# A hybrid encoder layer on one core: the stores of the local attention's output issued by POOL instead of SP

## The chip, the core and the metric

The kernel runs on one core of one Trainium2 chip. The metric is the device time of one launch in microseconds (us), as the median of several runs. The engines are named as the profile names them: PE (TensorE; PEld is its weight load), DVE (VectorE), ACT (ScalarE), POOL (GpSimd) and SP (SyncE). Each engine works through its own list of instructions in the order in which they stand there, and waits at one whose semaphores have not come.

## The reference, cut to what matters

One layer of an encoder over 1024 tokens of width 1024, in float32. A mixer made of a windowed softmax attention and a bidirectional gated delta rule is followed by a cross-attention into 256 memory tokens and a SwiGLU block, each between norms and with a residual:

```python
proj = h @ w_in                                   # h = rms_norm(x)
aq, ak, av, dqkv, dgate, dalpha, dbeta = split(proj)
attn_o = _window_attention(rope(aq), rope(ak), av, sink)   # 8 heads of 64, 2 kv heads, +-128 tokens
dn_o = _gated_deltanet(dqkv, dgate, dalpha, dbeta, ...)    # 4 heads, two directions, a scan over chunks
mix = concat([attn_o, dn_o], -1) @ w_out
x = x + rms_norm(mix)
x = x + rms_norm(cross_attention(rms_norm(x), rms_norm(mem)))
x = x + rms_norm(swiglu(rms_norm(x)))
```

The change touches `attn_o` on its way to the product with `w_out`.

## The kernel before, in words

Everything is computed transposed, with channels on the partitions, and matrices that do not fit are kept in DRAM scratch (names beginning with `d_`). Precision comes from splitting each float32 operand into a rounded high part and a rest (`split`, L103 on ACT and L104 on DVE or POOL) and multiplying three times.

The program is written as stages whose steps are interleaved by three lists of tokens. `ORDER_1` makes keys, queries and values of the delta rule and what its scan needs (`d_kv`, `d_pz`). `ORDER_2` makes the attention's queries and keys (L795, L797, into `d_q` and `d_k`) and begins the windows. `ORDER_3` runs the delta scan: `s01` is one quarter-by-quarter step of the two scans `scan(0)` and `scan(1)`, one for each pair of heads; `W` calls `next_windows`; `K` and `V` project the memory tokens. Then come the output projection (`mid_gemm`, L1104) over the first and the second half of the tokens, the cross-attention and the SwiGLU block.

A window is one token tile n of 128 tokens and one group g of four heads, 16 in all. `window(n, g)` is a generator in two halves. Its first half loads the tile's queries twice (`qr`, L674, SP), rounds them (`qs`, L676, ACT), replaces the lower 64 partitions by the rest (L677, POOL), multiplies with up to three key blocks (`psw`, L685, PE), adds the band and takes the row maximum (`sc`, `m`, L687, DVE), takes the exponential (L694, ACT), makes the sink's share (`es`, L697 on POOL, L698 on ACT, L699 and L700 on DVE) and scales (`sc`, L703 on DVE; in five of the windows L705 on ACT). The second half transposes (`ptw`, L711, PE), splits (`ph`, `pl`), multiplies with the values (`pow`, L716, PE), joins the two halves (`ao`, L719 on ACT, L720 on DVE) and stores the result to its place in `d_mix` (L721). `next_windows` runs the first half of one window, and then the second half of the one before. There is one `ao` tile and one `qr` tile.

A step of the scan loads `kv` (512 KB a direction, L858) and `pz` (L859) on SP, and runs products on PE (`psc`, L843) between which DVE updates `kv` (L871), `vg` (L878) and the state `S` (L891). From the fifth step on POOL adds and scales the two directions' outputs (`ol`, L920 to L930); `gate` (L918) is loaded and `osq` stored to `d_mix` (L940) on SP. In `next_keys` POOL makes the low part of the weights (`wlo`, L104). The output projection reads `d_mix` back (L1146).

All DMAs but the eight stores of `d_gate` (L817, ACT) are issued by SP. What stands behind what on an engine is not written by hand: a list scheduler goes through the recorded program with its own estimate of durations and places each instruction on its engine's list. DMAs issued by SP rotate through eight semaphores, so that each waits for the one issued eight before it.

Of the kernel before, what the change touches and what calls it, by code (L numbers as in the profile page):

```python
# [76 lines left out]
def tile_hybrid_block(  # L77
# [6 lines left out]
    nc = tc.nc  # L84
# [9 lines left out]
    def f32(ap):  # L94
        return ap.bitcast(F32)
# [4 lines left out]
    def split(hi, lo, src, scale=None, eng=None):  # L100

        if scale is None:
            nc.scalar.copy(hi, src)  # L103
            return (eng or nc.vector).tensor_tensor(lo, src, f32(hi), ALU.subtract)  # L104
        nc.scalar.activation(hi, src, AF.Identity, scale=scale)
        return nc.vector.scalar_tensor_tensor(lo, src, scale, f32(hi), ALU.mult, ALU.subtract)
# [83 lines left out]
    d_mix = dram.tile([D, S], F32, name="d_mix")  # L190
# [32 lines left out]
    for hf in range(2):  # L223
# [12 lines left out]
        for k in range(KT):  # L236
# [3 lines left out]
            g = gcol[:, k:k + 1]  # L240
# [422 lines left out]
    def window(n, g):  # L663

        tok = slice(n * P, (n + 1) * P)
        k0, k1 = max(n - 1, 0), min(n + 1, NT - 1) + 1
        nb = k1 - k0
        w = nb * P
        band = C[:, _AT["band0"] - C0 + (k0 - n + 1) * P:][:, 0:w]

        khi, klo = (t[:, k0 * P:k1 * P] for t in keys[g])
        qr = tw.tile([P, 4, P], F32, tag="qr", name="qr", bufs=1)
        for r in range(2):
            nc.sync.dma_start(qr[64 * r:64 * r + 64], d_q[256 * g:256 * g + 256, tok].rearrange("(h e) t -> e h t", h=4))  # L674
        qs = tw.tile([P, 4, P], F32R, tag="qs", name="qs")
        nc.scalar.copy(qs, qr)  # L676
        nc.gpsimd.tensor_tensor(qs[64:128], qr[64:128], f32(qs[64:128]), ALU.subtract)  # L677

        m4 = tw.tile([P, 4], F32, tag="m4", name="m4")
        ssum = tw.tile([P, 4], F32, tag="ssum", name="ssum")  # L680
        pr = []
        for hh in range(4):
            pp = pw.tile([P, 512], F32, tag="pw", name="psw")
            for i, kk in enumerate((khi, klo)):
                nc.tensor.matmul(pp[:, 0:w], qs[:, hh, :], kk, start=(i == 0), stop=(i == 1))  # L685
            sc = tw.tile([P, 384], F32, tag="sc", name="sc", bufs=8)
            nc.vector.tensor_tensor_reduce(out=sc[:, 0:w], in0=pp[:, 0:w], in1=band, scale=0.125,  # L687
                                           scalar=sink[:, 4 * g + hh:4 * g + hh + 1], op0=ALU.add, op1=ALU.max,
                                           accum_out=m4[:, hh:hh + 1])
            pr.append(sc)  # L690
        nm = tw.tile([P, 4], F32, tag="nm", name="nm")
        nc.vector.tensor_scalar(nm, m4, -1.0, None, ALU.mult)
        for hh in range(4):
            nc.scalar.activation(pr[hh][:, 0:w], pr[hh][:, 0:w], AF.Exp, bias=nm[:, hh:hh + 1],  # L694
                                 accum_out=ssum[:, hh:hh + 1])
        es = tw.tile([P, 4], F32, tag="es", name="es")
        nc.gpsimd.tensor_tensor(es, sink[:, 4 * g:4 * g + 4], m4, ALU.subtract)  # L697
        nc.scalar.activation(es, es, AF.Exp)  # L698
        nc.vector.tensor_tensor(es, es, ssum, ALU.add)  # L699
        nc.vector.reciprocal(es, es)  # L700
        for hh in range(4):
            if not 8 <= g * NT + n < 13:
                nc.vector.tensor_scalar(pr[hh][:, 0:w], pr[hh][:, 0:w], es[:, hh:hh + 1], None, ALU.mult)  # L703
            else:
                nc.scalar.mul(pr[hh][:, 0:w], pr[hh][:, 0:w], es[:, hh:hh + 1])  # L705
        yield
        po = pw.tile([P, 4, P], F32, tag="pow", name="pow", bufs=1)
        for j in range(nb):
            pp = pw.tile([P, 512], F32, tag="pw", name="ptw")
            for hh in range(4):  # L710
                nc.tensor.transpose(pp[:, hh * P:(hh + 1) * P], pr[hh][:, j * P:(j + 1) * P], ident)  # L711
            ph = tw.tile([P, 512], F32R, tag="ph", name="ph")
            pl = tw.tile([P, 512], F32R, tag="pl", name="pl")
            split(ph, pl, pp)
            for i, pe_ in enumerate((ph, pl)):
                nc.tensor.matmul(po.rearrange("p h t -> p (h t)"), vhl[:, k0 + j, g].rearrange("p r e -> p (r e)"), pe_,  # L716
                                 start=(j == 0 and i == 0), stop=(j == nb - 1 and i == 1))
        ao = tw.tile([P, 4, P], F32, tag="ao", name="ao", bufs=1)[0:64]
        nc.scalar.copy(ao, po[64:128])  # L719
        nc.vector.tensor_tensor(ao, po[0:64], ao, ALU.add)  # L720
        nc.sync.dma_start(d_mix[g * 256:(g + 1) * 256, tok].rearrange("(h e) t -> e h t", e=64), ao)  # L721

# [9 lines left out]
    def next_windows():  # L734

        for _ in range(2):
            last = wins[-1] if wins else None
            if wins_done[0] % NT == 0 and wins_done[0] < 2 * NT:
                window_keys(wins_done[0] // NT)
            if wins_done[0] < 2 * NT:  # L740
                wins.append(window(wins_done[0] % NT, wins_done[0] // NT))
                next(wins[-1])
            wins_done[0] += 1
            if last:
                next(last, None)
# [1131 lines left out]
```

## Time and profile before

| | |
|---|---|
| runs | 1518.25, 1521.06, 1524.97 us; median 1521.06 |
| profiled execution | 1518.84 us, of which the profile's span is 1516.8 us; mean granted clock of PE 0.996 |
| busy, share of the span | PE 97%, PEld 82%, DVE 73%, ACT 52%, POOL 24% |
| DMA | 256 MB in all, 169 GB/s on average; SP's queue 252.9 MB, ACT's 2.1 MB |

A row of the timeline has the start and the length in us, engine, line, operation and tiles; a number in brackets is how long the engine stood idle before it, with what released it. SPq is SP's queue of DMA issues: such a row is the issue, not the transfer. "Waits" rows give the idle time in total, the number of times and the longest. A busy PE is not a PE at its peak, since the ends of pipelined matmuls are modelled. The row of a stretch of the span has its start and end, its length, then the busy time of PE, PEld, DVE, ACT and POOL with the number of instructions in brackets, the clock granted to PE, the mean busy share of the 16 DMA engines, and GB/s.

### The profile page before, as it was taken

The numbers are of one execution on the slowest core, as the hardware profiler recorded it, in microseconds if no ns is written. First come the engines' busy times: TensorE is split into PE (matmuls) and PEld (weight loads), VectorE is DVE, ScalarE is ACT, GpSimd is POOL, SyncE is SP. The second block draws the span as 40 slices with busy tenths as digits, with TensorE's granted clock in tenths as the row PEclk, the third lists the DMA queues.
The fourth block names the chain that finished last, engine by engine and source line by source line (L and its number), as shares of the span: only waits on it lengthen the run. The fifth ranks groups of instructions, "written<-read, shape, count | busy, mean of one in ns | idle before, by whom it ended". The sixth has DMA issues, their size and how long they took to land.

```text
span 1516.8 us, 21323 instructions
## 1 busy us (share of the span) xinstructions
PE 1471.5 (97%) x7437; PEld 1239.2 (82%) x7437; DVE 1101.3 (73%) x1801; ACT 784.2 (52%) x1606; POOL 362.8 (24%) x394
## 2 busy tenths in 40 slices
PE   7999999998999999999999998999999999999998
PEld 6888877888989878887788876888888888888787
DVE  5878998676998775538466867776867764696666
ACT  7678844567556764555454684332332332453533
POOL 0011232432325303342201002433524342000030
PEclk9999999999999999999999999999999999999999
DMA  6245554557987584448625553334434333853255
GB/s 203 70 118 142 148 164 129 157 171 193 345 283 234 180 293 158 162 151 262 232 90 180 194 190 123 118 119 132 132 112 152 126 103 116 323 207 97 105 179 168
DMA packets 257751, 256.34 MB, mean 169 GB/s; under 512 B 18128, under 2 KB 190317, under 8 KB 257645
## 3 DMA queue, kind: packets, MB, share of 16 engines
q1 hardware_dynamic: 256493, 252.90, 52.3%
q10 hardware_dynamic: 1152, 2.10, 0.4%
q8 instruction: 58, 0.95, 0.3%
q14 instruction: 48, 0.39, 0.1%
HBM read 178.63 MB, written 73.70 MB: 166 GB/s over the span
## 4 chain that ended last, share of the span: by engine, by line
PE 64%; DVE 8%; DMA 5%; ACT 2%; issue 2%; POOL 1%; SPq 0%; DVEq 0%; ACTq 0%; POOLq 0%
PE pE L1514 8%; PE pD L1514 8%; PE pA L1514 6%; PE pmg L1104 6%; PE pdX L1720 6%; PE pst L1320 5%; PE pdA L1720 4%; PE pB L1514 4%; PE pcq L276 3%; PE psc L843 2%; PE pdD L1720 2%; DMA wpart<-in_w_co_dram 1%; PE pg L276 1%; DMA kv<-d_kv 1%; PE pcv L999 1%
## 5 line engine op out<-in xcount | busy, mean ns | idle before, releaser
L103 ACT CAST whi<-wraw 128x1024 fp32r<-128x1024 f32 x96 | 100.8, 1050 | 120.3 <-DMA wraw<-in_w_gate_up_dram 38.7
L276 PE MATMUL pg<-hlo,whi 128*128 128x512 f32 x352 | 140.0, 398 | 0.0
L276 PE MATMUL pg<-hhi,whi 128*128 128x512 f32 x352 | 139.4, 396 | 0.0
L276 PE MATMUL pg<-hhi,wlo 128*128 128x512 f32 x352 | 139.0, 395 | 0.0
L104 POOL TENSOR_TENSOR wlo<-wraw,whi 128x1024 fp32r<-128x1024 f32 x36 | 87.8, 2441 | 186.4 <-ACT whi L103 182.8
L1514 PE MATMUL pA<-b,whi 128*128 128x512 f32 x352 | 109.8, 393 | 3.6 <-ACT m L1541 2.8
L104 DVE TENSOR_TENSOR wlo<-wraw,whi 128x1024 fp32r<-128x1024 f32 x60 | 74.7, 1245 | 42.2 <-ACT whi L103 38.2
L1514 PEld LDWEIGHTS pA<-b,whi 128*128 128x128 f32 x352 | 65.2, 188 | 18.7 <-ACT m L1541 4.1
L1720 PE MATMUL pdX<-dhl,whi 128*128 128x512 f32 x264 | 76.1, 390 | 1.5 <-ACT dhl L103 0.8
L276 PEld LDWEIGHTS pg<-hhi,whi 128*128 128x128 f32 x352 | 66.5, 189 | 13.4 <-ACT hhi L241 0.3
L276 PEld LDWEIGHTS pg<-hlo,whi 128*128 128x128 f32 x352 | 66.5, 189 | 12.5
L276 PEld LDWEIGHTS pg<-hhi,wlo 128*128 128x128 f32 x352 | 66.5, 189 | 12.5
L1597 POOL TENSOR_TENSOR act<-act,up 128x512 f32<-128x512 f32 x33 | 51.0, 1546 | 82.0 <-DVE up L1596 60.9
L103 ACT CAST whi<-araw 128x1024 fp32r<-128x1024 f32 (+1 forms) x36 | 35.3, 981 | 67.1 <-PE pdX L1720 27.6
L1514 PE MATMUL pA<-b,wlo 128*128 128x512 f32 x176 | 68.8, 392 | 0.5 <-DVE wlo L104 0.5
L104 DVE TENSOR_TENSOR wlo<-araw,whi 128x1024 fp32r<-128x1024 f32 (+1 forms) x36 | 40.7, 1131 | 36.2 <-ACT whi L103 36.1
L1569 POOL TENSOR_TENSOR sr<-wraw 128x512 f32<-128x512 f32 x22 | 29.9, 1359 | 150.6 <-DMA wraw<-in_w_gate_up_dram 88.6
L301 DVE SCALAR_TENSOR_TENSOR acc<-cp,cols,acc 128x1024 f32<-128x1024 f32 x48 | 63.0, 1314 | 0.2
L1720 PEld LDWEIGHTS pdX<-dhl,whi 128*128 128x128 f32 x264 | 49.3, 188 | 12.7 <-ACT dhl L103 1.1
L103 ACT CAST dhl<-b 128x512 fp32r<-128x512 f32 x66 | 40.4, 620 | 31.9 <-PE pdA L1720 13.6
L1514 PE MATMUL pB<-s0h,s1h 128*128 128x512 f32 x176 | 54.4, 390 | 0.7 <-ACT s1h L103 0.7
L103 ACT CAST s0h<-sr 128x512 fp32r<-128x512 f32 x22 | 13.7, 622 | 78.7 <-POOL sr L1569 78.2
(503 smaller groups left out, 4306.1 us busy)
## 6 DMA issues: line engine op xcount, KB each, us to landing
wraw<-in_w_gate_up_dram SPq DMA_DIRECT2D x54, 512.0 KB, 3.8
kv<-d_kv SPq DMA_DIRECT2D x32, 512.0 KB, 7.2
wraw<-in_w_in_dram SPq DMA_DIRECT2D x22, 512.0 KB, 4.0
b<-in_w_down_dram SPq DMA_DIRECT2D x20, 512.0 KB, 6.3
araw<-d_as SPq DMA_DIRECT2D x20, 512.0 KB, 3.6
pz<-d_pz SPq DMA_DIRECT2D x32, 256.0 KB, 6.6
wraw<-in_w_ckv_dram SPq DMA_DIRECT2D x16, 512.0 KB, 4.7
wraw<-in_w_out_dram SPq DMA_DIRECT2D x16, 512.0 KB, 4.5
```

Source lines behind the costliest of these rows:

```text
L103: nc.scalar.copy(hi, src)
L104: return (eng or nc.vector).tensor_tensor(lo, src, f32(hi), ALU.subtract)
L276: nc.tensor.matmul(p_, w[:, k, :], ah[a][:, k, :], start=(k == 0 and i == 0), stop=(k == nk - 1 and i == 2))
L301: nc.vector.scalar_tensor_tensor(acc, cp[:, t:t + S], taps[t], acc, ALU.mult, ALU.add)
L843: nc.tensor.matmul(out[:, d, h, :], lt[:, d, h, :], rt[:, d, h, :], start=True, stop=True)
L999: nc.tensor.matmul(pp[t], mT[a][:, k, t * P:(t + 1) * P], w[:, kk, :], start=(k == 0 and i == 0), stop=(k == KT - 1 and i == 2))
L1104: nc.tensor.matmul(pp[t], act[a][:, k, tt], w_[:, kk, :], start=(k == 0 and i == 0), stop=(k == KT - 1 and i == 2))
L1320: nc.tensor.matmul(bank, a[:, tt], w, start=(start and i == 0), stop=(stop and i == 2), skip_group_check=not check)
L1514: nc.tensor.matmul(out_, w[a][:, k, :], xx[b_][:, k, :], start=(start and k == 0 and i == 0), stop=(k == HK - 1 and i == 2), skip_group_ch ...
L1569: nc.gpsimd.tensor_tensor(s[0], b_[:, 0:HK], b_[:, HK:], ALU.add)
L1597: nc.gpsimd.tensor_tensor(o_, o_, up, ALU.mult)
L1720: nc.tensor.matmul(banks[t], a[:, k - k0, tt], w, start=(first and k == 0 and i == 0), stop=(k == NB - 1 and i == 2), skip_group_check=not ...
```

## The change

The store at the end of `window` is issued by POOL instead of SP:

```diff
         nc.scalar.copy(ao, po[64:128])
         nc.vector.tensor_tensor(ao, po[0:64], ao, ALU.add)
-        nc.sync.dma_start(d_mix[g * 256:(g + 1) * 256, tok].rearrange("(h e) t -> e h t", e=64), ao)
+        nc.gpsimd.dma_start(d_mix[g * 256:(g + 1) * 256, tok].rearrange("(h e) t -> e h t", e=64), ao)
```

Each of the 16 stores moves 64 partitions x 4 heads x 128 tokens, 128 KB. They use semaphores of their own, and no longer one of SP's eight. The scheduler orders all engines anew between the first store and the middle of the output projection; ahead of and behind that the lists are the same, and no instruction is added or dropped.

On SP's list, at the first step of the second scan (`d_kv_104` and `d_pz_108` belong to `scan(1)`; `d_pz_108<-Z` is the last piece of what the scan needs):

```order
 L659 DMA d_pz_108<-Z_2199 128x4x128
 L859 DMA pz<-d_pz_108 128x512
-L721 DMA d_mix<-ao 64x4x128
 L858 DMA kv<-d_kv_104 128x1024 x2
 L730 DMA kraw<-d_k 64x1024
```

The two loads of `kv` now stand directly behind the load of `pz`, and the store between them is gone. The first of them waits there for PE alone (its place belonged to tiles that PE's projections read).

On POOL's list, in the middle of the scan (the number in `m_` tells the windows apart: 4204, 4274 and 4472 follow each other), before:

```order
L677 TENSOR_TENSOR qs<-qr,qs 64x512
L697 TENSOR_TENSOR es<-prm,m_4204 128x4
L677 TENSOR_TENSOR qs<-qr,qs 64x512
L697 TENSOR_TENSOR es<-prm,m_4274 128x4
L920 TENSOR_TENSOR ol<-ol,of 128x256 x2
L677 TENSOR_TENSOR qs<-qr,qs 64x512
L697 TENSOR_TENSOR es<-prm,m_4472 128x4
```

and now:

```order
L721 DMA d_mix<-ao 64x4x128
L697 TENSOR_TENSOR es<-prm,m_4204 128x4
L677 TENSOR_TENSOR qs<-qr,qs 64x512
L721 DMA d_mix<-ao 64x4x128
L697 TENSOR_TENSOR es<-prm,m_4274 128x4
L677 TENSOR_TENSOR qs<-qr,qs 64x512
L920 TENSOR_TENSOR ol<-ol,of 128x256 x4
L927 TENSOR_SCALAR ors<-oss 128x4
L721 DMA d_mix<-ao 64x4x128
L677 TENSOR_TENSOR qs<-qr,qs 64x512
L697 TENSOR_TENSOR es<-prm,m_4472 128x4
```

A store stands ahead of each `qs`, and `es` of window 4274 has moved ahead of the `qs` of window 4472 that it followed.

On DVE's list, from the row maximum of window 3549 on, before:

```order
L692 TENSOR_SCALAR nm<-m_3549 128x4
L871 SCALAR_TENSOR_TENSOR kv<-psc,nEG,kv 128x128 x4
L699 TENSOR_TENSOR es<-es,ssum 128x4
L700 RECIPROCAL es<-es 128x4
L703 TENSOR_SCALAR sc<-sc,es 128x384 x4
L104 TENSOR_TENSOR pl<-ptw,ph 128x512
L878 TENSOR_TENSOR vg<-psc,EG 128x512
L871 SCALAR_TENSOR_TENSOR kv<-psc,nEG,kv 128x128 x3
```

and now:

```order
L692 TENSOR_SCALAR nm<-m_3549 128x4
L871 SCALAR_TENSOR_TENSOR kv<-psc,nEG,kv 128x128 x4
L104 TENSOR_TENSOR pl<-ptw,ph 128x512
L699 TENSOR_TENSOR es<-es,ssum 128x4
L104 TENSOR_TENSOR pl<-ptw,ph 128x512
L871 SCALAR_TENSOR_TENSOR kv<-psc,nEG,kv 128x128 x4
L700 RECIPROCAL es<-es 128x4
L878 TENSOR_TENSOR vg<-psc,EG 128x512
L687 ISA sc,m_3906<-psw,C,prm 128x384
L687 ISA m_3906 128x1
L104 TENSOR_TENSOR pl<-ptw,ph 128x512
L703 TENSOR_SCALAR sc<-sc,es 128x384 x4
```

The scaling of window 3549 (L703) has moved behind two updates of the scan, three `pl` and the next window's first maximum.

## The prediction

> **What bounds the kernel now.** I read the page's first two parts for the engine that is never idle, then the busy time by stretches to find where that engine does wait, then SP's own waits, since the change takes 16 DMA issues from SP's queue, and last the timelines at the places where those issues stand.
>
> ```profile
> span 1516.8 us, 21323 instructions
> PE 1471.5 (97%) x7437; PEld 1239.2 (82%) x7437; DVE 1101.3 (73%) x1801; ACT 784.2 (52%) x1606; POOL 362.8 (24%) x394
> ```
>
> PE (TensorE) is busy in 1471.5 of 1516.8 us, so the end moves only by what PE's idle time grows or shrinks, or by its clock. The 16 stores of ao are issued between 321 and 554 us. The stretches there and just behind (stretch and its length, then busy us of PE, weight load, DVE, ACT, POOL, then granted clock, busy share of the DMA engines, GB/s):
>
> ```profile
> 310.00:360.00 50.00, 49.62 (x289) 42.96 (x288) 33.39 (x83) 33.77 (x75) 14.23 (x32) 1.00 0.52 153
> 360.00:400.00 40.00, 35.44 (x262) 32.80 (x260) 31.64 (x85) 26.68 (x61) 9.15 (x8) 0.96 1.00 303
> 400.00:440.00 40.00, 37.47 (x293) 36.28 (x293) 36.57 (x95) 20.23 (x45) 11.92 (x8) 0.96 0.97 318
> 560.00:600.00 40.00, 40.00 (x178) 33.14 (x177) 24.55 (x26) 20.61 (x35) 12.10 (x16) 1.00 0.53 185
> 600.00:640.00 40.00, 40.00 (x194) 33.46 (x194) 20.10 (x25) 19.68 (x35) 8.94 (x9) 1.00 0.42 135
> ```
>
> Up to 360 PE hardly waits (0.4 us). From 360 to 440, where the delta scan runs beside the windows, it waits 4.6 and 2.5 us, the DMA engines are full, and DVE is busy in 36.6 of 40 us from 400 on. From 560 to 640 PE has no gap. So the change can act on the end between 360 and 550 only. What SP waits for at the line of the store (total us, times, longest):
>
> ```profile
> SPq L721 <- DVE m L687: 13.4, 3, 10.3
> SPq L721 <- DVE mT L106: 5.5, 1, 5.5
> ```
>
> These two groups, the largest, hold SP for 18.9 us. Such a wait costs something only where a transfer stood ready behind the store and somebody waited for it.
>
> **The change part by part.**
>
> *SP without the stores: the head of the queue.* One of those waits is of that kind. The rows of SP, DVE and PE there:
>
> ```profile
> 355.47 0.33 SPq L859 DMA_DIRECT2D pz<-d_pz  x1
> 360.97 0.62 SPq L721 DMA_DIRECT2D d_mix<-ao  x1
> 361.70 1.01 SPq L858 DMA_DIRECT2D kv<-d_kv  x2
> 365.05 0.59 SPq L858 DMA_DIRECT2D kv<-d_kv  x1
> ...
> 360.26 0.68 DVE L720 TENSOR_TENSOR ao<-pow,ao 64x512 f32<-64x512 f32 x1
> ...
> 358.14 0.39 PE L276 MATMUL pg<-hhi,wlo 128*128 128x512 f32 x1
> 365.98 0.46 PE L843 MATMUL psc<-kv,pz 128*128 128x128 f32 x2 [1.84 <-issue]
> 376.25 0.68 PE L843 MATMUL psc<-S,kv 128*128 128x128 f32 x4 [1.27 <-DMA kv<-d_kv]
> ```
>
> After 355.80 SP stands still until DVE has made ao (360.94), then stores it and loads kv of the second scan's first step. PE has idled 1.84 us when it starts on that kv at 365.98. Without the store, this load waits for PE alone, and the last matmul of the projections, whose tiles give up their place, ends at 358.53. So the load can leave at 358.5 in place of 361.7, 3.2 us earlier, and the gap of 1.84 us closes. The loads behind it come up less, since kraw waits for other work of PE; of the 1.27 us at 376.25 I count half, 0.6. Gain: between 1.8 (this gap alone) and 3.2 (all that follows moves up); I take 1.84 + 0.6 = 2.4 us. The clock lies low in the same place:
>
> ```profile
> 365.00:370.00 5.00, 4.02 (x18) 3.75 (x19) 2.39 (x5) 4.24 (x11) 0.20 (x1) 0.67 1.07 249
> 420.00:430.00 10.00, 9.82 (x69) 9.64 (x70) 9.65 (x32) 3.90 (x10) 1.48 (x2) 0.83 0.79 261
> ```
>
> If it came back to 1.00, that would be 0.33 x 5 = 1.65 us more in the first row; I leave this for the faster rival. The longest wait of SP, 10.3 us until 344.59, is worth nothing: it lies in the stretch where PE is busy in 49.62 of 50 us.
>
> *SP's issue time.* One issue takes 0.602 us:
>
> ```profile
> L721 SPq DMA_DIRECT2D d_mix<-ao x16: 586/602/836, 321.0 to 554.3; - x16
> DMA to landing us min/median/max: 2.5/2.8/6.3
> ```
>
> 16 x 0.602 = 9.6 us leave SP, at no gain: SP is not on PE's path except where it blocks a load, which is counted. On this the Trainium skill ("DMA: Bandwidth & Descriptors", section "Issuing engines are not separate DMA queues") speaks against the change: issuing from several engines saves the sequencer's issue time alone. By that rule the gain is 0 in place of 2.4; the rows above agree about the issue time, but show that the queue also loses the wait at its head. I keep it as a rival.
>
> *POOL with the stores: their length.* No DMA issued by POOL is in the trace. From below its cost is 0; from above the longest landing, 6.3 us. The nearest row is POOL's own operation on a block of the same 64x512 elements:
>
> ```profile
> L677 POOL TENSOR_TENSOR qs<-qr,qs 64x512 fp32r<-64x512 f32 x12 | 15.4, 1282 | 44.7 <-ACT qs L676 31.9 <-DVE m L687 7.2 <-ACT es L698 3.1
> ```
>
> I take 1.3 us. 16 x 1.3 = 21 us on an engine with 24% busy. What counts is what stands behind a store on POOL: qs of a later window, for which PE waits (psw, L685). Three places, with DVE's end of ao, POOL's qs and PE's first use of that qs:
>
> ```profile
> 396.26 0.67 DVE L720 TENSOR_TENSOR ao<-pow,ao 64x512 f32<-64x512 f32 x1
> 402.59 0.28 PE L685 MATMUL psw<-khi,qs 128*128 128x256 f32 x1
> ...
> 424.26 0.68 DVE L720 TENSOR_TENSOR ao<-pow,ao 64x512 f32<-64x512 f32 x1
> 430.74 0.34 PE L685 MATMUL psw<-khi,qs 128*128 128x384 f32 x1
> ...
> 438.93 0.67 DVE L720 TENSOR_TENSOR ao<-pow,ao 64x512 f32<-64x512 f32 x1
> 439.09 1.27 POOL L677 TENSOR_TENSOR qs<-qr,qs 64x512 fp32r<-64x512 f32 x1 [10.75 <-ACT qs L676]
> 441.31 0.20 POOL L697 TENSOR_TENSOR es<-prm,m 128x4 f32<-128x4 f32 x1 [0.94 <-DVE m L687]
> 442.16 0.34 PE L685 MATMUL psw<-khi,qs 128*128 128x384 f32 x1
> ```
>
> At the first, store and qs end at 396.93 + 1.3 + 1.28 = 399.5, before 402.59: hidden. At the second, with es between them, at 424.94 + 1.3 + 0.2 + 1.28 = 427.7, before 430.74: hidden. At the third the new order of POOL (in the section on the change) puts the store and es of the window before ahead of qs; es waits for DVE until 441.31, so qs ends at 441.51 + 1.27 = 442.8, and PE is 0.6 us late. Loss: 0.6 us.
>
> *DVE beside POOL.* DVE's scaling of sc (L703) does not run beside a long operation of POOL:
>
> ```profile
> 400.92 1.39 DVE L703 TENSOR_SCALAR sc<-sc,es 128x384 f32<-128x384 f32 x4
> 414.84 5.02 DVE L703 TENSOR_SCALAR sc<-sc,es 128x256 f32<-128x256 f32 x4
> ...
> 414.46 4.74 POOL L104 TENSOR_TENSOR wlo<-wraw,whi 128x1024 fp32r<-128x1024 f32 x2 [2.75 <-ACT whi L103]
> ```
>
> Four narrower ones take 5.02 us while POOL splits two weight tiles, against 1.39 alone: 3.6 us lost. The Trainium skill ("SBUF — State Buffer", section "Who interferes with whom") names this lock for DVE's copies and tensor_scalar, and says that a DMA issued by POOL meets it too, when it writes its descriptors. By that rule every store beside an L703 would cost DVE up to the store's length. In the rows L703 begins 4.0 us behind the end of ao (396.93 to 400.92), so a store of 1.3 us is over: 0 us, and up to 2.3 us at this place with 6.3 us.
>
> *ao's buffer and the end.* There is one ao tile, so ACT's next copy waits until the store has landed. The closest two windows:
>
> ```profile
> 546.89 0.68 DVE L720 TENSOR_TENSOR ao<-pow,ao 64x512 f32<-64x512 f32 x1 [1.33 <-ACT ao L719]
> 551.30 0.59 ACT L719 COPY ao<-pow 64x512 f32<-64x512 f32 x1
> 553.60 0.68 DVE L720 TENSOR_TENSOR ao<-pow,ao 64x512 f32<-64x512 f32 x1
> ```
>
> With 1.3 us on POOL and 2.8 to land it is there at 547.57 + 4.1 = 551.7, and the copy ends at 552.3, before DVE turns to it at 553.60. The loads of d_mix behind the last store feed the second half of the output projection, and PE is full until 640: 0 us.
>
> The sum: -2.4 + 0.6 = -1.8 us. The profiled execution took 1518.84 us (its span of 1516.8 and 2.0 around it), so it would take 1517.0. It lies 2.2 us below the median of the three runs (1521.06), which would come to **1519.3 us**, 0.1% down. Some 0.5%, 7.6 us, is what a measurement of this kernel can tell from no change.
>
> **The rivals.**
>
> *Faster: the whole crowded stretch moves up.* If the earlier start frees all that PE waits for from 360 to 440, and the clock stays up, the gain is 4.56 + 2.53 + 1.65 + 0.17 x 10 = 10.4 us: 1510.7. For it: DMA engines full at 1.00 and 0.97 but only 0.52 before 360, so loads that leave earlier find room. Against it: part of the waits in 400 to 440 is DVE's 5.02 us above, which the change does not touch.
>
> *No change: only issue time is saved*, since kv's place is released later than I read it: 1521.
>
> *Slower: a store holds POOL for long.* With 6.3 us each, the three places make PE late by 396.93 + 6.3 + 1.28 - 402.59 = 1.9, by 424.94 + 6.3 + 0.2 + 1.28 - 430.74 = 2.0, and by 439.60 + 6.3 + 0.2 + 1.27 - 442.16 = 5.2, and L703 by 2.3: 11.4 less 2.4, so +9.0 and 1530. It outweighs the gain from about 3.5 us a store (then 0, 0 and 2.4). For it: POOL is the slower engine on equal blocks; against it: SP issues the same store in 0.6.
>
> *Slower: the new order holds back a window.* The rows between 310 and 610 are ordered anew on every engine. In DVE's new order (section on the change) L703 of one window stands behind three pl, the second scan's update of kv, a vg and a sc, which all stood behind it:
>
> ```profile
> L104 DVE TENSOR_TENSOR pl<-ptw,ph 128x512 fp32r<-128x512 f32 x36 | 24.3, 679 | 0.7 <-ACT ph L103 0.6
> L878 DVE TENSOR_TENSOR vg<-psc,EG 128x512 f32<-128x512 f32 x14 | 9.3, 678 | 0.5 <-PE psc L843 0.4
> L687 DVE CUSTOM_DVE_ANT_0 sc<-psw,C,prm 128x384 f32<-128x384 f32 x34 | 20.5, 608 | 9.4 <-PE psw L685 9.2
> 437.89 1.12 DVE L871 SCALAR_TENSOR_TENSOR kv<-psc,nEG,kv 128x128 f32<-128x128 f32 x4
> ```
>
> That is 3 x 0.68 + 1.12 + 0.68 + 0.61 = 4.4 us later for this window's transposes (ptw), and PE takes its rows in order. One such wait uncovered outweighs the gain; three in the stretch where DVE is full make 13.2 - 2.4 + 0.6 = +11.4, so 1532.5. Against it: the scan gains there what the window loses (its second update no longer stands behind L703, 1.39 us in the row above), and other places exchange the other way.
>
> **How the numbers follow.** Forecast (within 2 us of 1519.3): 0.30. Only issue time: 0.07. Faster rival: 0.24. Long stores: 0.18. New order: 0.21, of which 0.03 stay within 0.5%. So faster by over 0.5% 0.24, within 0.40, slower 0.36. The range goes from 1508, a little past the faster rival, to 1534, past both slower ones; the forecast's own is 1515 to 1524.
>
> **What would show it.** The 16 stores on POOL's row instead of SP's, and their length: 1.3 us or nearer to 6. kv of the second scan's first step issued near 358.5 and PE's gap of 1.84 us gone. psw near the three places late by less than 1 us. L703 at 1.4 us but for the one beside the weight split. PE's idle time from 360 to 440 near 5 us, not 7. For the new order: PE's waits for sc and pl of DVE. The prediction is wrong if PE's idle time from 440 to 550 grows, if a store takes over 3.5 us, or if the stretch past 640 changes its length.

## The result, and the profile after

The changed kernel takes **1515.86 us** (median, 1512.52 to 1521.33), the kernel before in the same rounds 1520.95 (1513.9 to 1524.97). The ratio is 0.9969, 95% interval [0.9957, 0.998]: 4.7 us or 0.31% faster (3.0 to 6.5 us). The prediction said 1519.3, 1.8 us faster. The profiled execution of after took 1518.03 us, 2.2 above its median, while that of before lay 2.1 below its own; so the two traces are compared stretch by stretch and not by their ends.

The page of after, its span and its engines:

```profile
span 1516.3 us, 21329 instructions
PE 1472.7 (97%) x7437; PEld 1239.5 (82%) x7437; DVE 1099.3 (72%) x1801; ACT 783.8 (52%) x1606; POOL 374.2 (25%) x410
```

POOL has gained 11.4 us, and PE is as full as it was. By stretches (columns as in the prediction), after:

```profile
360.00:400.00 40.00, 36.89 (x285) 34.28 (x285) 35.28 (x97) 26.87 (x62) 11.27 (x11) 1.00 0.95 308
400.00:440.00 40.00, 39.27 (x318) 37.79 (x317) 36.56 (x98) 20.34 (x47) 12.76 (x11) 1.00 1.01 315
440.00:480.00 40.00, 37.45 (x257) 34.28 (x256) 31.04 (x77) 29.86 (x90) 24.74 (x32) 1.00 0.80 254
```

PE's idle time from 360 to 440 falls from 7.1 us to 3.11 + 0.73 = 3.8, and the clock of both rows goes from 0.96 to 1.00. From 440 to 480 idle time appears: 2.55 us, where before has 0.73:

```profile
440.00:480.00 40.00, 39.27 (x283) 36.25 (x283) 34.52 (x88) 30.43 (x90) 20.10 (x30) 1.00 0.81 255
```

The rows of after at the place of the prediction's first term (SP, then PE, then DVE and POOL):

```profile
356.91 0.90 SPq L858 DMA_DIRECT2D kv<-d_kv  x2
...
364.13 0.66 PE L711 MATMUL ptw<-ident,sc 128*128 128x128 f32 x4 [0.38 <-DVE m L687]
375.96 0.45 PE L685 MATMUL psw<-khi,qs 128*128 128x384 f32 x1 [2.14 <-DVE m L687]
...
371.25 3.52 DVE L703 TENSOR_SCALAR sc<-sc,es 128x384 f32<-128x384 f32 x4
414.70 1.14 DVE L703 TENSOR_SCALAR sc<-sc,es 128x256 f32<-128x256 f32 x4
...
371.43 2.47 POOL L104 TENSOR_TENSOR wlo<-wraw,whi 128x1024 fp32r<-128x1024 f32 x1 [5.54 <-ACT whi L103]
417.04 2.37 POOL L104 TENSOR_TENSOR wlo<-wraw,whi 128x1024 fp32r<-128x1024 f32 x1 [5.19 <-ACT whi L103]
```

The kv loads leave at 356.91, no store stands ahead of them, and the two gaps of PE at 365.98 and 376.25 are gone. A new one of 2.14 us at 375.96 follows from an L703 that in the new order runs beside POOL's weight split (3.52 us instead of 1.4). The other L703, which took 5.02 us at 414.84, is now over before the split begins: 1.14 us. Two things therefore changed at once, a queue and an order, and the trace cannot say which of them paid. The stores themselves, on POOL:

```profile
L721 POOL DMA_DIRECT2D d_mix<-ao x16: 622/644/872, 322.5 to 549.4; - x16
DMA to landing us min/median/max: 2.7/5.3/6.4
```

0.644 us each, nearly what SP took (0.602); the landing takes 5.3 us instead of 2.8.

Where the time stands further on: the first matmul of the SwiGLU, in before and then in after.

```profile
L1514 PE MATMUL pA<-b,whi x352: 387/389/507, 864.3 to 1292.2; 128*128 128x512 f32 x176
```

```profile
L1514 PE MATMUL pA<-b,whi x352: 387/389/628, 859.9 to 1290.8; 128*128 128x512 f32 x176
```

After is 4.4 us ahead when it starts and 1.4 when it ends. No order differs there. Over the first 85.7 us of this group PE's clock is 0.96 in after and 1.00 in before, which is 0.04 x 85.7 = 3.4 us. The timed runs keep the 4.7 us, so I put those 3 us down to this one execution.

### The profile page after: what moved, and what is told of

Same layout as the page of the kernel before. It is cut to its first block, busy times and chain, and to the rows that moved or that the text cites. A ratio compares the mean times of both kernels' runs of the same rounds, so it can differ in the third digit from the quotient of the medians.

```text
span 1516.3 us, 21329 instructions
## 1 busy us (share of the span) xinstructions
PE 1472.7 (97%) x7437; PEld 1239.5 (82%) x7437; DVE 1099.3 (72%) x1801; ACT 783.8 (52%) x1606; POOL 374.2 (25%) x410
## 4 chain that ended last, share of the span: by engine, by line
PE 76%; DVE 9%; DMA 7%; ACT 2%; issue 2%; SPq 1%; POOL 0%; DVEq 0%; ACTq 0%; POOLq 0%
PE pg L276 11%; PE pE L1514 8%; PE pD L1514 8%; PE pA L1514 6%; PE pmg L1104 6%; PE pdX L1720 6%; PE pst L1320 5%; PE pB L1514 4%; PE pcq L276 3%; PE psc L843 3%; PE pdA L1720 2%; PE pdD L1720 2%; DMA b<-in_w_down_dram 1%; DMA wpart<-in_w_co_dram 1%; PE pco L1219 1%
```

## The experiments

**Theory Q** (queue): a store that waits for ao holds the loads behind it on SP; the gain is that kv's loads are freed. **Theory R** (rows): the engine that issues is immaterial, the gain comes with the new order of PE, DVE and ACT rows. **Theory N**: only issue time goes, worth nothing.

A scheduler makes the order anew after every edit, so an edit alone can change more than it says. Most kernels below therefore hold the order: the names of the instructions in the order of before (or after) are listed for each engine, and an edge puts each behind the one listed ahead of it. Such an edge adds no wait. The first four hold the stretch in which before and after differ (1200 rows of PE, 384 of DVE, 279 of ACT, 30 of POOL, 103 to 181 of SP), the later ones nearly the whole program. Gains are the ratio times the median of before in the same rounds.

```
+def _pin(nc, tc):
+    traced = {i.name: i for i in nc.cur_bb.bb.instructions}
+    for row in _ROWS:
+        names = [f"I-{n}" for n in row.split()]
+        for a, b in zip(names, names[1:]):
+            tc.add_manual_dep(traced[b], a, DependencyInfo(NoSync, DATA), reason="row")
```

### The order of before, stores on POOL

```
-        nc.sync.dma_start(d_mix[...], ao)
+        nc.gpsimd.dma_start(d_mix[...], ao)
 rows of PE, DVE, ACT and the other rows of POOL and SP: as before
```

> The order of before is held on PE, DVE, ACT and for all else on SP and POOL; only the 16 stores go to POOL. Theory Q (the queue: kv of the second scan no longer stands behind a store that waits for ao): the gap of 1.84 us at 365.98 goes and part of the 1.27 us at 376.25, so -2.4 us against before (-1.8 to -3.2), kv issued near 357 and the L703 at 414 still long (near 5 us) beside two wlo, with the 2.41 us gap at 420 left. Theory R (the rows that the new order moves on PE, DVE and ACT carry the gain): 0 to -0.6 us, all of the -5 us missing. Theory N (only SP's issue time is saved): 0 us.

Measured: 1516.71 us, ratio 0.9974 [0.9961, 0.9987], -4.0 us (-5.9 to -2.0). With not one row of PE, DVE or ACT moved the gain is there, and the intervals can't tell it from that of the change. Its timelines, SP and then PE and DVE:

```profile
357.90 0.90 SPq L858 DMA_DIRECT2D kv<-d_kv  x2
...
374.99 0.44 PE L685 MATMUL psw<-khi,qs 128*128 128x384 f32 x1 [0.28 <-DVE m L687]
419.37 1.74 PE L843 MATMUL psc<-kv,pz 128*128 128x128 f32 x8 [3.33 <-DVE kv L871]
...
414.05 5.01 DVE L703 TENSOR_SCALAR sc<-sc,es 128x256 f32<-128x256 f32 x4
```

The two gaps behind kv are gone; the slow L703 at 414 and the gap behind it have stayed, as they must in this order.

### The order of after, stores on SP

```
 nc.sync.dma_start(d_mix[...], ao)
 rows of PE, DVE, ACT and the other rows of POOL and SP: as after
```

> The order of after is held on PE, DVE, ACT and for all else on SP and POOL; only the 16 stores stand on SP again, the third of them ahead of the kv loads of the second scan as in before. Theory Q: the gain of the queue is lost, so the kernel stands at -2.3 us or less against before (what the place of the L703 beside wlo gives), and PE waits about 1.8 us for the late kv near 366. Theory R: nearly all of the gain of after stays, -4.5 us. Theory N: -4.5 us as well, since issue time is free.

Measured: 1521.73 us, ratio 1.0007 [0.9993, 1.002], +1.1 us (-1.1 to +3.0). All of the gain is lost. The store is back at the head, and PE waits for kv:

```profile
364.43 0.61 SPq L721 DMA_DIRECT2D d_mix<-ao  x1
365.15 1.01 SPq L858 DMA_DIRECT2D kv<-d_kv  x2
...
369.57 0.90 PE L843 MATMUL psc<-kv,pz 128*128 128x128 f32 x4 [1.97 <-issue]
458.10 2.04 PE L843 MATMUL psc<-kv,pz 128*128 128x128 f32 x14 [1.57 <-DVE kv L871]
...
376.29 1.40 DVE L703 TENSOR_SCALAR sc<-sc,es 128x384 f32<-128x384 f32 x4
420.75 1.14 DVE L703 TENSOR_SCALAR sc<-sc,es 128x256 f32<-128x256 f32 x4
```

Theory R falls with these two runs: the new order alone is worth nothing that can be measured. I had expected that it would keep some 2.3 us for the better place of the L703 at 414. That group is short here too (1.14 us, at 420.75), and the one that took 3.52 us in after takes 1.40 us, because POOL's split begins behind it (at 378.02). So neither group loses time here, and the kernel still gains nothing. Part of what the order loses is the wait of 1.57 us at 458.10 and one of 0.84 us for ACT's ph at 447.23, which before does not have and after has too (1.90 and 0.65); the rest is not found. It also follows that the 3.52 us of after do not come from the order alone, but from the order with kv early.

### The order of before, one swap on SP

```
 SP, rows of before:
-L721 DMA d_mix<-ao 64x4x128
 L858 DMA kv<-d_kv_104 128x1024 x2
+L721 DMA d_mix<-ao 64x4x128
```

> The kernel before with one swap on SP: the third store stands behind the two kv loads of the second scan's first step instead of ahead of them; all other rows of all engines as before, POOL issues no store. Theory Q: the same gain as the old order with all stores on POOL, -2.4 us (-1.8 to -3.2), the gap at 366 gone. Theory R and theory N: 0 us.

Measured: 1516.79 us, ratio 0.9975 [0.9965, 0.9985], -3.8 us (-5.3 to -2.3). POOL issues nothing here; two rows of one queue changed places, and that gives what the change gives, within the intervals. The two waits of PE for kv are gone:

```profile
354.39 0.90 SPq L858 DMA_DIRECT2D kv<-d_kv  x2
359.50 0.62 SPq L721 DMA_DIRECT2D d_mix<-ao  x1
...
362.51 0.39 PE L843 MATMUL psc<-kv,pz 128*128 128x128 f32 x2
370.37 0.61 PE L843 MATMUL psc<-S,kv 128*128 128x128 f32 x4
```

### The order of before, the other 15 stores on POOL

```
-        nc.sync.dma_start(d_mix[...], ao)
+        (nc.sync if g * NT + n == 2 else nc.gpsimd).dma_start(d_mix[...], ao)
```

> The order of before is held; 15 stores go to POOL and the third, the one ahead of the kv loads of the second scan, stays on SP where it stood. Theory Q in its narrow form (that one store alone): 0 us, the gap of 1.84 us at 366 stays and POOL's 15 stores of 0.64 us cost nothing. If other stores blocked loads too: -0.5 to -2 us, with gaps behind 440 shorter. If POOL's stores cost: +0.5 us or more.

Measured: 1520.71 us, ratio 0.9996 [0.9978, 1.0013], -0.6 us (-3.3 to +2.0). So neither a gain from 15 of the 16 moves nor a cost of POOL's 15 issues shows; only their sum is measured, and to some 3 us. The third store still holds kv, and PE still waits for it:

```profile
361.52 0.62 SPq L721 DMA_DIRECT2D d_mix<-ao  x1
362.23 1.03 SPq L858 DMA_DIRECT2D kv<-d_kv  x2
...
366.33 0.46 PE L843 MATMUL psc<-kv,pz 128*128 128x128 f32 x2 [1.64 <-DMA kv<-d_kv]
```

### The order of before, kv three rows later

```
 SP, rows of before:
 L721 DMA d_mix<-ao 64x4x128
-L858 DMA kv<-d_kv_104 128x1024 x2
 L730 DMA kraw<-d_k 64x1024
 L125 DMA wraw<-in_w_ckv_dram 128x8x128
 L730 DMA kraw<-d_k 64x1024
+L858 DMA kv<-d_kv_104 128x1024 x2
```

> The kernel before with one move on SP the other way: the two kv loads of the second scan's first step stand three rows later, behind the two kraw loads and the wraw load, so that by the rows of before they leave near 365.1 instead of 361.70. Theory Q, one us late is one us lost: +3.3 us (+2 to +4). If the store's queue time costs only by the idle it makes and other work fills it: 0 to +1. If the loads behind them, which now leave 1 us earlier, matter as much: near 0 or below.

Measured: 1525.97 us, ratio 1.0036 [1.0021, 1.0052], +5.5 us (+3.2 to +7.9). The dose works in the other direction too, and more than one for one. Counted from the first matmul of memory's transposes (ptm, L968: 359.5 in before, 362.8 here), kv left 4.3 us behind it (367.07) instead of 2.2, so 2.1 us later, and PE stood for 6.32 us in one piece, 4.5 us more than in before. Three loads stand ahead of kv here, and the run does not tell their part from that of the later issue.

```profile
373.78 0.76 PE L843 MATMUL psc<-kv,pz 128*128 128x128 f32 x2 [6.32 <-DMA kv<-d_kv]
```

### The order of before, stores on ACT

```
-        nc.sync.dma_start(d_mix[...], ao)
+        nc.scalar.dma_start(d_mix[...], ao)
```

> The order of before, all 16 stores issued by ACT. Theory Q says that what a waiting store blocks is its own queue: SP is freed (-4.4 us, as with one swap on SP), but ACT, which has next to no slack between 360 and 550, now waits for ao at each store: ACT copies half of ao itself and DVE's add of 0.6 us with its queue ahead of it follows, so 1 to 3 us of ACT's time at several of the 16. In all -2 to +6 us, most likely +1. If the engine that issues were immaterial: -4.4 us, as POOL.

Measured: 1528.19 us, ratio 1.0044 [1.0027, 1.0061], +6.7 us (+4.1 to +9.3). SP is freed as with POOL (kv leaves at 358.38), and the time goes up by more than that saves. ACT, DVE and PE at the worst place, and PE's clock and the DMA share behind it (last three columns):

```profile
382.87 0.61 ACTq L721 DMA_DIRECT2D d_mix<-ao  x1
383.53 0.61 ACT L694 ACTIVATE sc<-sc,nm 128x384 f32<-128x384 f32 x1 [6.76 <-DMA pz<-d_pz]
...
375.92 0.69 DVE L720 TENSOR_TENSOR ao<-pow,ao 64x512 f32<-64x512 f32 x1
...
387.07 0.80 PE L716 MATMUL pow<-ph,vhl 128*128 128x512 f32 x1 [5.05 <-ACT ph L103]
...
392.00:394.00 2.00, 2.00 (x10) 1.90 (x10) 1.23 (x5) 0.00 (x0) 0.00 (x0) 0.50 0.00 2
```

ao was ready at 376.61; the store stood on ACT until 382.87 all the same, and the profile names the landing of a pz load as what released it; why a store should wait for that load, the trace does not say. Behind it stood four exponentials and the two ph casts for which PE then waited 5.05 us. So an issue that waits at the head of ACT's list holds ACT's own work, as one on SP holds loads. That I had set the likeliest value at +1 was wrong in size: I had counted the wait for ao only, and this wait is another. It was also wrong that ACT has next to no slack: in before it is busy in 26.7 of the 40 us from 360 and in 20.2 of those from 400.

### The order of before, each store in two halves on POOL

```
-        nc.sync.dma_start(d_mix[g * 256:(g + 1) * 256, tok]..., ao)
+        [nc.gpsimd.dma_start(d_mix[g * 256 + 128 * r:][:128, tok]..., ao[:, 2 * r:2 * r + 2]) for r in range(2)]
```

> The order of before, each store on POOL cut into two halves of 64 KB: 32 issues on POOL instead of 16, the same bytes. Theory: a store of 0.64 us on POOL is hidden, so 16 more (10 us of POOL) cost nothing: the time of the old order with 16 stores on POOL, -4.4 us, within 1 us. If POOL's time is on the path: 0.64 us for each of the stores that has work right behind it, 4 to 8 of them, so -4.4 + 3 to 5 = about 0 us.

Measured: 1519.61 us, ratio 0.9984 [0.9967, 1.0001], -2.4 us (-5.0 to +0.2). It lies between the two expectations and decides neither. PE's waits from 355 to 560 are those of 16 whole stores (10.4 us in both), but the output projection has a new one:

```profile
L721 POOL DMA_DIRECT2D d_mix<-ao x32: 590/607/861, 322.2 to 553.9; - x32
...
566.10 0.80 PE L1104 MATMUL pmg<-whi,s0h 128*128 128x512 f32 x1 [2.41 <-ACT whi L103]
...
SPq L1146 <- DMA d_mix<-ao: 8.3, 2, 7.5
```

The loads of d_mix (L1146) waited 7.5 us at the head of SP for the last half, and weight loads stood behind them. In after this wait is 6.2 us, in before 3.8, and no gap of PE follows.

### The same, the last store whole on SP

```
+        nc.sync... if g * NT + n == 15 else two halves on nc.gpsimd
```

> The order of before, 15 stores as two halves each on POOL, the 16th whole on SP at its old place. Theory E (the halves lost what they did at the end: the last half left late and landed 7 us later, the d_mix loads waited for it at the head of SP, the weight loads behind them came late, PE idled 2.41 us at 566): without it the time is that of 16 whole stores on POOL, -4.4 us (-3 to -6), and no PE gap between 560 and 570. If POOL's own time is what the halves cost: about -1.2 us as with 32 halves.

Measured: 1520.22 us, ratio 0.9987 [0.9973, 1.0001], -2.0 us (-4.1 to +0.2). The gap of the projection is gone in the profile,

```profile
560.00:570.00 10.00, 10.00 (x46) 8.29 (x45) 8.12 (x10) 7.34 (x14) 0.00 (x0) 1.00 0.55 195
```

but the time did not come back: theory E is not borne out as the cause. Against 16 whole stores on POOL, 16 more issues cost some 2 us by the two ratios, with intervals that overlap; what they cost, and where, stays open.

### The order of before, the gap filled with matmuls

```
             pv = bank()
+            if g == 1 and step == 0: 12 x nc.tensor.matmul(pv[:, 0, 0, :], ident, ident, start=True, stop=True)
```

> The kernel before, with 12 extra matmuls of 128x128 on PE right ahead of the first matmul that waits for the late kv, written into the bank that this one then overwrites: 12 x 0.115 = 1.4 us of the 1.84 us gap at 364.1 is filled, nothing comes earlier. Clock theory: the half clock that the rows of before show from 366 to 370 (0.67 and 0.50, 1.7 us lost) follows from the idle, so it stays at 1.00 and the time falls by 1.7 us though not one us of the wait is removed. Without it (the clock has other reasons): 0 us, or +0.5 where the extra matmuls come late.

Measured: 1522.85 us, ratio 1.0008 [0.999, 1.0026], +1.2 us (-1.5 to +4.0). The 12 matmuls took twice what I had counted (24 records, 362.50 to 365.18), 0.7 us past the gap. The clock did stay up:

```profile
366.00:368.00 2.00, 2.00 (x19) 1.87 (x18) 1.05 (x2) 1.80 (x7) 0.00 (x0) 1.00 1.18 246
...
L968 PE MATMUL ptm<-ident,mt x16: 271/273/273, 358.0 to 359.7; 128*128 128x128 f32 x16
L843 PE MATMUL psc<-S,kv x224: 270/275/372, 374.2 to 506.2; 128*128 128x128 f32 x112
```

The same two groups in before, and in the kernel with the swap:

```profile
L968 PE MATMUL ptm<-ident,mt x16: 271/273/273, 359.5 to 361.2; 128*128 128x128 f32 x16
L843 PE MATMUL psc<-S,kv x224: 270/275/377, 376.2 to 507.1; 128*128 128x128 f32 x112
```

```profile
L968 PE MATMUL ptm<-ident,mt x16: 271/272/273, 358.1 to 359.7; 128*128 128x128 f32 x16
L843 PE MATMUL psc<-S,kv x224: 270/275/275, 370.4 to 501.5; 128*128 128x128 f32 x112
```

From ptm to the first matmul on S it is 16.7 us in before, 16.1 with the gap filled and the clock full, 12.3 with the swap. Of the 1.7 us that the full clock saved, 0.7 went to the matmuls that ran past the gap, and at 374 PE waited 1.64 us for the next kv instead of 1.27; 0.6 us is left. With gap and clock mended PE still waits for a load, so the loads set this stretch, not PE, its gap or its clock. The timed runs agree, though narrowly: their interval ends at -1.5 us, short of the 1.7.

### The order of before, four scalings of window 7 on ACT

```
-            if not 8 <= g * NT + n < 13:
+            if not 7 <= g * NT + n < 13:
 ACT: whi, then the four L705, then whi; all other rows as before, stores on SP
```

> The kernel before, all stores on SP, all orders held; only the four scalings L703 of window 7 (the group that took 5.02 us at 414.84 beside POOL's two wlo) move from DVE to ACT, where they stand between the two weight casts of that place. Theory W (the weight split on POOL slows that group, and this is a second loss of its own, apart from the store): the gap of 2.41 us at 420.18 goes, ACT takes 4 x 0.45 = 1.8 us in a stretch in which it idles 5.5 us: -2 to -3.5 us against before. If the group is slow for another reason or ACT's late second cast takes its place: 0 to +2 us.

Measured: 1515.74 us, ratio 0.9959 [0.9946, 0.9973], -6.2 us (-8.2 to -4.1), more than expected. POOL's split stands where it stood and takes as long; the four scalings run beside it on ACT in 1.70 us, and PE has no gap there. The gap in before and the clock behind it, and then the rows of this run:

```profile
420.18 1.27 PE L843 MATMUL psc<-kv,pz 128*128 128x128 f32 x8 [2.41 <-DVE kv L871]
420.00:425.00 5.00, 4.82 (x25) 4.68 (x26) 5.00 (x18) 1.17 (x2) 0.00 (x0) 0.66 1.08 368
```

```profile
414.05 1.70 ACT L705 ACTIVATE sc<-sc,es 128x256 f32<-128x256 f32 x4
...
414.29 4.86 POOL L104 TENSOR_TENSOR wlo<-wraw,whi 128x1024 fp32r<-128x1024 f32 x2 [2.74 <-ACT whi L103]
...
415.00:420.00 5.00, 5.00 (x39) 4.56 (x39) 4.05 (x13) 3.20 (x7) 4.06 (x2) 1.00 1.08 289
```

The gap of 2.41 us and the half clock behind it, 0.34 x 5 = 1.7 us, come to 4.1 us, which the interval just includes. I had counted the gap alone; the other 2.1 us I can't place.

### Both edits in the order of before

```
 the swap on SP, and the four scalings of window 7 on ACT
```

> Both edits in the order of before: the third store behind the two kv loads on SP, and the four scalings of window 7 on ACT. If the two losses are independent the gains add up: -4.4 - 2.4 = -6.8 us (-5 to -8), about 1514, a kernel faster than both. If the DMAs between 365 and 420 are the bound behind both: -4.4 us as with the swap alone.

Measured: 1515.26 us, ratio 0.9952 [0.9933, 0.997], -7.3 us (-10.2 to -4.6). It is the fastest of the kernels here, but it can't be told from the scalings alone (-6.2), nor, by the intervals, from the changed kernel (0.9969). The gains do not add up to -10 in the median, though the interval reaches it; in the traces both effects are there (neither gap is left), and whether the sum truly falls short stays open.

### The changed kernel, the same scalings on ACT, order free

```
-            if not 8 <= g * NT + n < 13:
+            if not 7 <= g * NT + n < 13:
 in the changed kernel; all engines ordered anew
```

> The changed kernel (stores on POOL, its own free order) with the four scalings of window 7 on ACT; the order of the rest moves as well, and in it that group was already short (1.14 us at 414.70). Theory W: nothing left to gain there, so -4.7 us as the changed kernel, give or take 2 us for the rows that move. If it gives -7, the gain of the edit has another source than the weight split beside it.

Measured: 1523.95 us, ratio 1.0016 [1.0001, 1.0032], +2.4 us (+0.2 to +4.9): about 7 us slower than the changed kernel without it. PE's waits from 355 to 560:

```profile
PE psw L685 <- DVE m L687: 4.1, 3, 2.1
PE pow L716 <- ACT ph L103: 3.7, 2, 2.0
PE ptw L711 <- DVE m L687: 2.0, 2, 1.6
```

In after the first of these is 4.6, the second 0.7 and the third 0.4 us. The edit that gains 6.2 us in a held order comes with a loss of 7 when the order is made anew. The run changes the edit and the order together; but the group that the edit takes off DVE was already short here, and the waits that have grown are at other lines, so I put the loss down to the order, which is argued and not shown. It is then a finding, not a matter of course, that the new order that came with the change was worth nothing.

## Why the prediction was right in sign, and short in size

The kernel came out 4.7 us faster, not 1.8: outside the 2 us that I had given the forecast, and well short of the 10.4 of the faster rival. Of the 2.9 us that were missing, 1.4 belong to the first term (3.8 by the swap, not 2.4) and 0.6 to a loss on POOL that did not come; the remaining 0.9 are within the intervals.

**The head of SP's queue (-2.4): the right cause, mis-sized.** Measured alone it is -3.8 us (-5.3 to -2.3) by the swap, -4.0 with the stores on POOL in the old order, -4.7 with the new one. Two numbers were short. kv left not 3.2 us earlier but 5.4: in after 3.3 us ahead of the first ptm (356.91 to 360.17), in before 2.2 behind it (361.70 to 359.52). It left right behind the pz load, ahead of the last matmuls of the projections (until 359.2 in after); that it waits there for PE, as I had read, is not so. And I counted half of the second gap, on the view that the loads further back move little. The whole of it went. In before no DMA moved anything from 358 to 360 (share 0.00), and from 365 on they were full (1.07); this fits a queue that could not make up later what it held up at 357. The half clock from 366 to 370, 1.7 us, which I had left for the faster rival, is gone as well in after and with the swap; the filled gap shows that it is worth little by itself.

```profile
358.00:360.00 2.00, 2.00 (x14) 1.81 (x13) 1.27 (x4) 1.04 (x2) 0.00 (x0) 1.00 0.00 0
```

In the kernel with the swap the same stretch moves data at a share of 0.74. That the loads, not PE, set the place rests on the filled gap and on the dose.

**SP's issue time (0): right.** 15 stores off SP gave -0.6 us (-3.3 to +2.0). The rule of the Trainium skill that I weighed there ("DMA: Bandwidth & Descriptors", section "Issuing engines are not separate DMA queues") holds for those 15; the rival built on it (1521) fails by the sixteenth.

**POOL's stores (1.3 us, +0.6): too long, and the loss not seen.** The nearest row, POOL's own work on as many elements, was a poor measure of an issue: 0.644 us each. No wait of PE from 355 to 560 in after names POOL. With the 15 alone the time stays at before's. Twice as many issues seem to cost some 2 us, which is not settled; the break-even of 3.5 us a store was far off.

**DVE beside POOL (0): the step that failed.** I wrote that the change does not touch the 5.02 us of L703. It did, through the order: 1.14 us there, and 3.52 at another place. In the held order they stay (5.01). That leaving the term at 0 did no harm is luck. The group itself is worth -6.2 us in the order of before, but the order of after with the stores on SP, in which no L703 is slow, stands at +1.1 us (-1.1 to +3.0); so it loses about as much elsewhere, and only part of that is found (the waits at 447 and 458).

**ao's buffer and the end (0): right, with little in hand.** L1146 waits 6.2 us instead of 3.8 for the last store and PE has no gap; with 7.5 us it had one.

**The signs of being wrong.** Two of the three that I had named came true in the traces. PE's idle time from 440 to 550 grew, from 5.3 to 6.6 us: two waits there, 1.9 us for DVE's kv (L871) and 0.7 for ACT's ph, are not in before. They are in both traces of the new order and not in that of the old order with the stores on POOL, so they go with the new order. And the stretch past 640 got longer: after is 4.4 us ahead where the SwiGLU begins and 0.5 at the end of the span (1516.3 against 1516.8). Of these 3.9 us, 3.4 are the clock told above, so this sign says more of the one execution than of the change.

**The faster rival** asked for all waits from 360 to 440: half of them went, and the clock came back. **The new order** as a loss did not come with this change; the same kind of loss came with the scalings in free order (+2.4).

## What to carry to other kernels

Look for the instruction that waits at the head of a DMA queue while a ready load stands behind it, above all where the DMA engines idle ahead of a stretch in which they are full: a swap of two rows gave what moving 16 issues gave. Another engine's queue helps if that engine has nothing behind the waiting issue; on ACT the same move cost 6.7 us. Judge an edit with the order held, since in one case here an edit that gained 6.2 us with the order held came with a loss of 7 in a new one.

## What the runs showed of the hardware

- The issue takes about the same on each engine: 0.602 us on SP, 0.644 on POOL, 0.582 on ACT, and 0.607 on POOL for half the bytes. The landing was slower away from SP: 2.8 us on SP (before), 5.3 on POOL (after; 5.2 in the old order), 4.7 on ACT (medians).
- A tensor_scalar of DVE beside POOL's split takes 5.01 to 5.03 us for four of 128x256 instead of 1.14, in all nine traces that have that group on DVE in the order of before; DVE's update of kv (L871, scalar_tensor_tensor, one operand from PE's psc) is not slowed: with the scalings on ACT it takes 1.13 and 1.11 us beside the same split, and 1.12 alone.
- The clock falls to 0.50 behind some gaps of PE and not behind others: behind 1.84 us in before it did, from 366 to 370, behind 2.14 us in after it did not. The Trainium skill ("TensorE: Matmul & The Clock Gate", section "What's actually happening") has the clock follow how busy PE was in a window of some 3.4 us that runs freely; by my reading the same gap can then fall into it differently from run to run. The traces agree in the length: from 355 to 565 the clock lost comes in steps of 1.7 us, that is 3.4 us at half clock (none with 32 half stores, 1.71 us in after, 3.41 with the stores on POOL in the old order, 5.12 in before, 6.83 with the stores on ACT). What sets off a step no run here shows.
